# Norms of a diffusion trunk's first feed-forward block and of its mixing's input, set in steps among matrix products, with three modulations computed earlier

## The chip, the cores and the metric

The kernel runs on one core of a Trainium2 chip. The metric is the time of one execution on the device, in microseconds (us). Instructions run on five engines: TensorE (PE, matrix products; PEld is its loading of weights), VectorE (DVE), ScalarE (ACT), GpSimd (POOL) and SyncE (SP, which here issues all loads and stores, in order). Each engine executes its own list of instructions in order, and waits on semaphores for what the others make.

## The reference, cut to what matters

One layer for 1024 latent tokens and 256 context tokens, model width 1024, feed-forward width 2816:

```python
def rms_norm(x, w):
    xf = x.astype(jnp.float32)
    y = xf * lax.rsqrt(jnp.mean(xf * xf, axis=-1, keepdims=True) + EPS)
    return (y * w.astype(jnp.float32)).astype(x.dtype)

def modulate(h, shift, scale):
    return h * (1.0 + scale[:, None, :]) + shift[:, None, :]

def swiglu(h, w1, w3, w2):
    return (jax.nn.silu(h @ w1) * (h @ w3)) @ w2
...
m_l = jnp.split(cond_lat @ ada_w[i] + ada_b[i], N_MOD, axis=-1)
m_c = jnp.split(cond_ctx @ ada_w[i] + ada_b[i], N_MOD, axis=-1)
x = x + 0.5 * m_l[2] * swiglu(modulate(rms_norm(x, norm1_w[i]), m_l[0], m_l[1]), ffn1_w1[i], ffn1_w3[i], ffn1_w2[i])
ctx = ctx + 0.5 * m_c[2] * swiglu(modulate(rms_norm(ctx, norm1_w[i]), m_c[0], m_c[1]), ffn1_w1[i], ffn1_w3[i], ffn1_w2[i])
y_l, y_c = token_mixing(modulate(rms_norm(x, norm2_w[i]), m_l[3], m_l[4]),
                        modulate(rms_norm(ctx, norm2_w[i]), m_c[3], m_c[4]), w_in[i], ...)
x = x + m_l[5] * y_l
x = x + 0.5 * m_l[8] * swiglu(modulate(rms_norm(x, norm3_w[i]), m_l[6], m_l[7]), ffn2_w1[i], ffn2_w3[i], ffn2_w2[i])
return rms_norm(x, final_norm_w)
```

`m_l` and `m_c` hold nine modulations of 1024 values each, for latent and context tokens. The context needs modulations 0 to 4 alone; the latents use 5 on the way out of the mixing, 6 and 7 in the norm before the second feed-forward block (FFN2), and 8 in FFN2.

## The kernel before

All arithmetic is in float32. Each operand of a product is split into a high and a low part (`split`: ACT makes the high part, L58, DVE or POOL subtracts it, L59), and each product is three matmuls: high by high, low by high and high by low (`mm3`, L63 to L65). Weights come through a ring of six raw tiles (NR), loaded at L232, and a ring of six pairs `whi`, `wlo` (NH). Activations lie transposed, features over the 128 partitions, tokens along the row: x as eight tiles k of 128 features for each token group, which are latent half 0, latent half 1 (512 tokens each) and the context (256).

The first feed-forward block (FFN1) of the latents uses a scheme of seven products in place of eight for each 2 by 2 block of matrices. **Phase 1** (`hidden`, up to about 475 us) makes the hidden tiles, two of the 22 at a time, in chains of seven products of 12 matmuls, and writes seven combinations of them to memory. Between the chains it computes modulations (`mods`, MPER reductions a time): a column of a modulation is one load of 512 KB (`ada`) and one reduction on DVE over 1024 values (L104), with low priority in the scheduler, for latents and context alike when both need it. Modulations 0 and 1 of the latents are done by the start, and phase 1 makes 2, 4 and 3 for both and 1 and 0 for the context.

The **second phase** (`back6`, up to about 690 us) reads these combinations (`gd`) and weights (`w2` blocks, or sums of them, `sd`) back. It does products 1, 2, 6, 5, 7 and 3, in this order, of eleven steps each; a step is 12 matmuls of 512 columns with one pair of split operands (`whi`, `wlo` for the weights, `hh`, `hl` for the activations) into four banks of PSUM (`psa` or `psb`). Products 7 and 3 of these subtract two loaded blocks on DVE first (L364). Each step calls the generator `feed` once. `feed` loads the context's x in the first eight steps, then the latents' x again, one tile each two steps (L1354), and from the second quarter of x on also makes modulations 5, 7 and 6 in halves (`mods_half`): 24 columns in two halves of 512, each a strided load of 256 KB (L118) and a reduction (L119). After product 2 the function `ctx_in` norms the context, with its two norm matmuls lowered by 300 (LR1), so that they stand behind product 6 on PE.

A norm is: `squares` (ACT squares, L151 and L154; DVE adds up in `nacc`, L155), `rstd_col` (one narrow matmul for each 128 tokens sums over the partitions, L164; `pow_half` takes DVE, L913, and POOL, L914, for the power -1/2, tile `nr`), `rstd_rows` (DVE makes diagonal matrices `ndiag`, L174; a matmul with ones spreads them, L176; ACT copies, L183, tile `nrb`), and `norm_k` for each of the eight tiles (L191 on DVE, L192 on ACT, L193 on DVE).

Then comes the context's FFN1 in classic form (`classic`, 11 calls of two hidden tiles each, with POOL as the engine for low parts, and `Y`, which multiplies the hidden tiles back and adds to x, L531 and L544), up to about 901 us; product 4 of the latents, to 934; the context's keys and values for the mixing (`ctx_k`, `ctx_v`), to 970; then the mixing of the latents (`lat_phase`). The norms of the mixing's input lie in here: that of latent half 1 before `classic`, with a priority 100 lower for its part up to the spread, and one `norm_k` after each call of `classic`; that of the context after the last `Y`; that of latent half 0 after `ctx_k`, its `norm_k` after `ctx_v`.

The order of each engine's instructions is not that of the code alone: a scheduler places them by priority, where `high_priority` moves a stretch of the code ahead (a negative offset moves it back). `pair` and `load_half` load and split ahead of the products in this way.

## Time and profile before

| what | value |
| --- | --- |
| median of 3 runs | 2230.6 us (2229.64 to 2230.91) |
| profiled execution | 2230.59 us, its span 2228.1 us |
| mean granted PE clock | 0.989 |
| PE busy | 95% of the span, 11442 matmuls |
| DVE, ACT, POOL busy | 70%, 44%, 13% |
| HBM | 298.29 MB read, 66.09 MB written, 164 GB/s over the span |

A row of a timeline reads: start, duration, engine, line, operation, output<-inputs, shapes, how many were joined; in brackets the idle time of the engine before it and what released it. A row of the waits reads: engine, tile and line that waited, <- what it waited for: us in total, how many times, the longest. Matmul records overlap, so that their pace is read from start to start. Line numbers are those of the kernel before; the kernel after has the same statements a few lines off (its L165 and L177 are L164 and L176 here, L60 is L59, L64 to L66 are L63 to L65, L911 is L913, L175 is L174, L105 is L104, L360 is L364, L410 is L414).

### The profile page before, as it was taken

How to read it: one execution, taken by the hardware profiler on the slowest of the kernel's cores; microseconds unless marked ns; L12 is line 12 of the kernel's file. 1: busy time of each engine (PE TensorE's matmuls, PEld its weight loads, DVE VectorE, ACT ScalarE, POOL GpSimd, SP SyncE). 2: the span in 40 equal slices, each digit the busy share in tenths (PEclk: the TensorE clock that was granted, in tenths of full speed). 3: DMA queues.
4: the chain of work that ended last, by engine and by line, in shares of the span. 5: the costliest groups of instructions: out<-in, count | busy, mean ns of one | idle time of the engine just before them, and what ended most of it. 6: DMA issues, size and time to landing. Idle time of an engine off the chain costs nothing. (4 is left out here: it accounts for less than half of the span.)

```text
span 2228.1 us, 32714 instructions
## 1 busy us (share of the span) xinstructions
PE 2121.1 (95%) x11442; PEld 1800.6 (81%) x11442; DVE 1550.9 (70%) x2803; ACT 982.5 (44%) x1807; POOL 290.1 (13%) x294
## 2 busy tenths in 40 slices
PE   4999999999798999999998999999999999999998
PEld 3877888887687999888877888778878888888888
DVE  7999986665698745763567446766786766665686
ACT  3333344344344554555653445334444343444553
POOL 2000000000003665331032112300000000010000
PEclk9999999999999999999999999999999999999999
DMA  6558654468897566554322223324234444457674
GB/s 238 184 158 274 216 174 139 142 220 272 289 342 242 167 184 189 178 181 112 99 65 73 78 78 88 101 74 158 79 123 146 161 153 154 147 199 249 210 247 150
DMA packets 206822, 374.95 MB, mean 168 GB/s; under 512 B 24321, under 2 KB 37569, under 8 KB 206657
## 3 DMA queue, kind: packets, MB, share of 16 engines
q1 hardware_dynamic: 206656, 372.86, 51.7%
q8 instruction: 89, 1.46, 0.3%
q14 instruction: 77, 0.62, 0.1%
HBM read 298.29 MB, written 66.09 MB: 164 GB/s over the span
## 5 line engine op out<-in xcount | busy, mean ns | idle before, releaser
L58 ACT ACTIVATE whi<-raw 128x512 fp32r<-128x512 f32 (+1 forms) x659 | 406.6, 623 | 726.7 <-issue 219.3
L59 DVE TENSOR_TENSOR wlo<-raw,whi 128x512 fp32r<-128x512 f32 (+1 forms) x541 | 376.1, 698 | 312.3 <-ACT whi L58 305.1
L63 PE MATMUL psa<-hh,whi 128*128 128x512 f32 (+1 forms) x1432 | 526.7, 369 | 8.2 <-ACT hh L192 6.1
L65 PE MATMUL psa<-hh,wlo 128*128 128x512 f32 (+1 forms) x1432 | 527.0, 368 | 4.0 <-DVE wlo L59 2.1
L64 PE MATMUL psa<-hl,whi 128*128 128x512 f32 (+1 forms) x1432 | 527.7, 368 | 3.2 <-DVE hl L59 2.7
L63 PEld LDWEIGHTS psa<-hh,whi 128*128 128x128 f32 x1432 | 272.1, 190 | 51.7 <-ACT hh L192 7.2
L64 PEld LDWEIGHTS psa<-hl,whi 128*128 128x128 f32 x1432 | 272.6, 190 | 47.3 <-DVE hl L59 5.2
L65 PEld LDWEIGHTS psa<-hh,wlo 128*128 128x128 f32 x1432 | 272.5, 190 | 45.9 <-DVE wlo L59 2.5
L63 PE MATMUL psb<-hh,whi 128*128 128x512 f32 (+1 forms) x740 | 283.5, 385 | 6.8 <-ACT whi L58 2.5
L65 PE MATMUL psb<-hh,wlo 128*128 128x512 f32 (+1 forms) x740 | 284.0, 384 | 1.5 <-DVE wlo L59 1.5
L64 PE MATMUL psb<-hl,whi 128*128 128x512 f32 (+1 forms) x740 | 284.2, 384 | 0.8 <-DVE hl L59 0.8
L59 POOL TENSOR_TENSOR wlo<-raw,whi 128x512 fp32r<-128x512 f32 (+1 forms) x118 | 159.2, 1368 | 199.2 <-ACT whi L58 196.5
L63 PEld LDWEIGHTS psb<-hh,whi 128*128 128x128 f32 x740 | 139.5, 189 | 37.1 <-ACT whi L58 4.2
L65 PEld LDWEIGHTS psb<-hh,wlo 128*128 128x128 f32 x740 | 139.3, 188 | 30.6 <-DVE wlo L59 3.7
L64 PEld LDWEIGHTS psb<-hl,whi 128*128 128x128 f32 x740 | 139.6, 189 | 29.2 <-DVE hl L59 2.4
L914 POOL TENSOR_TENSOR nr<-nr,mhalf 128x4 f32<-128x4 f32 (+1 forms) x11 | 10.6, 963 | 883.8 <-DVE nr L913 880.7
L59 DVE TENSOR_TENSOR hl<-raw,hh 128x512 fp32r<-128x512 f32 x159 | 109.5, 694 | 9.8 <-ACT hh L58 9.5
L58 ACT ACTIVATE hh<-raw 128x512 fp32r<-128x512 f32 x159 | 97.0, 620 | 18.9 <-DMA raw<-gd 16.4
L64 PE MATMUL psa<-wlo,hh 128*128 128x256 f32 (+1 forms) x320 | 94.2, 294 | 0.2
L63 PE MATMUL psa<-whi,hh 128*128 128x256 f32 (+1 forms) x320 | 93.5, 292 | 0.0
L65 PE MATMUL psa<-whi,hl 128*128 128x256 f32 (+1 forms) x320 | 92.9, 290 | 0.0
L64 PEld LDWEIGHTS psa<-wlo,hh 128*128 128x128 f32 x320 | 62.2, 195 | 1.0 <-DVE wlo L59 0.9
(360 smaller groups left out, 3656.4 us busy)
## 6 DMA issues: line engine op xcount, KB each, us to landing
raw<-in_w SPq DMA_DIRECT2D x374, 256.0 KB, 3.1
gd<-s SPq DMA_DIRECT2D x154, 256.0 KB, 3.0
raw<-gd SPq DMA_DIRECT2D x154, 256.0 KB, 3.8
ada<-in_adaT SPq DMA_DIRECT2D x56, 512.0 KB, 4.3
s<-in_w SPq DMA_DIRECT2D x66, 256.0 KB, 4.5
s<-in_adaT SPq DMA_DIRECT2D x64, 256.0 KB, 5.1
sd<-s SPq DMA_DIRECT2D x44, 256.0 KB, 2.8
hh<-in_w SPq DMA_DIRECT2D x44, 256.0 KB, 4.5
```

The source lines that it names most:

```text
L58: nc.scalar.activation(hi, src, AF.Copy)
L59: (eng or nc.vector).tensor_tensor(out=lo, in0=src, in1=hi.bitcast(F32), op=ALU.subtract)
L63: mm(ps, wa[0], xa[0], start=start, stop=False, skip_group_check=more)
L64: mm(ps, wa[0], xa[1], start=False, stop=False, skip_group_check=more)
L65: mm(ps, wa[1], xa[0], start=False, stop=stop, skip_group_check=more)
L914: nc.gpsimd.tensor_tensor(out=r, in0=r, in1=self.mhalf[:, :n], op=ALU.pow)
```

## The change

Modulations 5, 7 and 6 join the list of phase 1 as 24 reductions of full width, and MPER goes from 4 to 6; the second phase makes none. `feed` follows a plan by step number: loads of x at the same steps as before, and steps of the norms. A norm is cut into steps: 0 the squares, 1 `rstd_col`, 2 `rstd_rows` with the copy, and one `norm_k` each. The context's first norm has its steps at 22 (the first of product 6, counted from 0), 24, 27 and 30 to 37; the second norm of latent half 1 has its squares before `classic` and one step after each of its calls; the last `Y` of the context's FFN1 and the context's second norm lie inside product 4, at its steps 1, 4, 6, 7 and 8; that of latent half 0 has its squares after product 4 and its next two steps inside `ctx_k`. The lowered priorities of these norms go. Product 4 uses the banks `psa` instead of `psb`, and the transposes of the gate columns in `ctx_v` get priority 60 lower.

```diff
-    def back6(self, mid=lambda: None, keep=True):
+    def back6(self, keep=True):
...
         self.add4(0, 0, self.plus4(c1, B))
-        mid()
         self.prod(6, A, False)
...
+        plan = defaultdict(list)
+        for k in range(KD):
+            plan[k].append(lambda k=k: self.load_x((None, None, hc), (2,), (k,)))
+        for i, (tg, k) in enumerate((tg, 4 * q + k) for tg, q in ((0, 0), (1, 1), (0, 1), (1, 0)) for k in range(4)):
+            o = TGS[tg][0]
+            plan[8 + 2 * i].append(lambda tg=tg, k=k, o=o: nc.sync.dma_start(self.x[tg][k], I["xT"][k * P:(k + 1) * P, o:o + 512]))
+        nrm = {}
+
+        def norm_step(tg, i, a, b):
+            n = TGS[tg][1]
+            if i == 0:
+                nrm[tg] = self.squares(self.x[tg], n, n2)
+            elif i == 1:
+                nrm[tg] = self.rstd_col(nrm[tg], n, n2)
+            elif i == 2:
+                pr = self.rstd_rows(nrm[tg], n, n2)
+                nrm[tg] = self.scr(n2, "nrb")[:, :n]
+                nc.scalar.copy(nrm[tg], pr)
+            else:
+                self.norm_k(tg, i - 3, a, b, nrm[tg], n2)
+
+        ctx1 = lambda i: norm_step(2, i, self.mcol(1, 1), self.mcol(0, 1))
+        norm2 = lambda tg, i: norm_step(tg, i, self.mcol(4, int(tg == 2)), self.mcol(3, int(tg == 2)))
+        for i, at in enumerate((22, 24, 27, *range(30, 30 + KD))):
+            plan[at].append(lambda i=i: ctx1(i))
+
+        CT = [(2, 0, 256)]
+        p4 = 6 * NP
+        plan[p4 + 1] += [lambda: self.Y(NF - 2, CT), lambda: self.alloc_h((2,), hc), lambda: norm2(2, 0)]
+        plan[p4 + 4].append(lambda: norm2(2, 1))
+        plan[p4 + 6].append(lambda: norm2(2, 2))
+        for k in range(KD):
+            plan[p4 + 7 + k // 4].append(lambda k=k: norm2(2, 3 + k))
+
         def feed():
-            for k in range(KD):
-                self.load_x((None, None, hc), (2,), (k,))
-                yield
-            late = self.mods_half(hc, LMODS)
-            for i, (tg, q) in enumerate(((0, 0), (1, 1), (0, 1), (1, 0))):
...
-        def ctx_in():
-            self.psN = self.psB
-            self.norm_mod(2, self.mcol(1, 1), self.mcol(0, 1), n2, LR1)
-
-        self.back6(ctx_in, False)
+            for i in range(7 * NP):
+                for go in plan[i]:
+                    go()
+                yield
+
+        self.feed = feed()
+        self.psN = self.psB
+        self.back6(False)
...
+        self.alloc_h((1,), self.hp)
+        norm2(1, 0)
+        pend = [lambda i=i: norm2(1, i) for i in range(1, 3 + KD)] + [lambda: spill(1)]
         for f in range(0, NF, 2):
             self.classic(f, (2,), mid=(lambda: self.Y(f - 2, CT)) if f else None, eng=[nc.gpsimd if e else None for e in CENG])
-            for _ in range(NPEND if f else 0):
-                if pend:
-                    pend.pop(0)()
-        self.Y(NF - 2, CT, after)
-        B = self.bank4(self.psB)
-        self.prod(4, B, True)
-        self.add4(0, 1, B)
-        after(0, 0, 512)
+            pend.pop(0)()
+        A = self.bank4(self.psA)
+        self.prod(4, A, True)
+        self.add4(0, 1, A)
+        self.alloc_h((0,), self.hp)
+        norm2(0, 0)
+        for i, _ in enumerate(self.ctx_k(f1)):
+            if i in (3, 5):
+                norm2(0, i // 2)
+        self.ctx_v(f1)
+        for k in range(KD):
+            norm2(0, 3 + k)
+        spill(0)
...
-EMODS = ((2, (0, 1)), (1, (1,)), (0, (1,)), (4, (0, 1)), (3, (0, 1)))
-LMODS = (5, 7, 6)
-MPER = 4
-LR1 = 300
+EMODS = ((2, (0, 1)), (1, (1,)), (0, (1,)), (4, (0, 1)), (3, (0, 1)), (5, (0,)), (7, (0,)), (6, (0,)))
+MPER = 6
...
-RP = (0, 100, 0)
-NPEND = 1
```

PE at the context's first norm, before: the last matmul of a step of product 6 (`psa`), the two norm matmuls (`psb` from `nacc` and from `ndiag`; one record stands for two), and the next step, of product 5 (`hh`, `hl` activations, `whi`, `wlo` weights).

```order
2302 L65 MATMUL psa_4066<-hh_1102_5004,wlo_5013 128x512
2303 L164 MATMUL psb_4682<-ones_88,nacc_4659 128x1 x2
2304 L176 MATMUL psb_4688<-ndiag_4689,ones_88 128x128
2305 L63 MATMUL psb_5040<-hh_1117_5044,whi_5052 128x512
2306 L64 MATMUL psb_5040<-hl_1118_5045,whi_5052 128x512
2307 L65 MATMUL psb_5040<-hh_1117_5044,wlo_5053 128x512
```

L164 and L176 are neighbours. After, the first norm matmul follows a step of product 6:

```order
2205 L65 MATMUL psa_4139<-hl_1048_4784,whi_4791 128x512
2206 L66 MATMUL psa_4139<-hh_1047_4783,wlo_4792 128x512
2207 L165 MATMUL psb_4808<-ones_88,nacc_4736 128x1 x2
2208 L64 MATMUL psa_4136<-hh_1055_4814,whi_4822 128x512
2209 L65 MATMUL psa_4136<-hl_1056_4815,whi_4822 128x512
2210 L66 MATMUL psa_4136<-hh_1055_4814,wlo_4823 128x512
```

and the second one stands 36 product matmuls further on, three steps later:

```order
2241 L64 MATMUL psa_4139<-hh_1067_4863,whi_4871 128x512
2242 L65 MATMUL psa_4139<-hl_1068_4864,whi_4871 128x512
2243 L66 MATMUL psa_4139<-hh_1067_4863,wlo_4872 128x512
2244 L177 MATMUL psb_4887<-ndiag_4888,ones_88 128x128
2245 L177 MATMUL psb_4887<-ndiag_4891,ones_88 128x128
2246 L64 MATMUL psa_4136<-hh_1077_4896,whi_4904 128x512
2247 L65 MATMUL psa_4136<-hl_1078_4897,whi_4904 128x512
```

The two matmuls, adjacent before, have three steps between them now.

DVE at the same place, before: `nr` and `ndiag` are the norm's, `wlo` and `hl` low parts for steps to come, L119 the half reductions.

```order
773 L119 ISA modl_80 128x1
774 L59 TENSOR_TENSOR wlo_5163<-raw_5160,whi_5162 128x512
775 L59 TENSOR_TENSOR hl_1132_5100<-raw_5101,hh_1131_5099 128x512
776 L913 TENSOR_SCALAR nr_4685<-psb_4682 128x2
777 L174 TENSOR_SCALAR ndiag_4689<-ident_92,nr_4685 128x128
778 L174 TENSOR_SCALAR ndiag_4692<-ident_92,nr_4685 128x128
779 L59 TENSOR_TENSOR wlo_5190<-raw_5187,whi_5189 128x512
780 L59 TENSOR_TENSOR hl_1139_5127<-raw_5128,hh_1138_5126 128x512
781 L119 ISA s_5029,modl_80<-s_5029,row_4508,cols_78 128x512
782 L119 ISA modl_80 128x1
```

After, with L360 a subtraction of weight blocks for product 7, and L410 the addition of product 2 to x:

```order
774 L60 TENSOR_TENSOR wlo_4930<-raw_4927,whi_4929 128x512
775 L60 TENSOR_TENSOR hl_1068_4864<-raw_4865,hh_1067_4863 128x512
776 L410 SCALAR_TENSOR_TENSOR x_862_4123<-s_4425,modl_80,x_862_4123 128x512
777 L360 TENSOR_TENSOR hh_1203_5371<-hh_1203_5371,hl_1204_5373 128x512
778 L911 TENSOR_SCALAR nr_4811<-psb_4808 128x2
779 L360 TENSOR_TENSOR hh_1210_5398<-hh_1210_5398,hl_1211_5400 128x512
780 L60 TENSOR_TENSOR wlo_4954<-raw_4951,whi_4953 128x512
781 L60 TENSOR_TENSOR hl_1078_4897<-raw_4898,hh_1077_4896 128x512
782 L175 TENSOR_SCALAR ndiag_4888<-ident_92,nr_4811 128x128
783 L175 TENSOR_SCALAR ndiag_4891<-ident_92,nr_4811 128x128
```

The half reductions are gone; `nr` stands behind splits, an addition and a subtraction, and `ndiag` behind one subtraction and two splits more.

PE at the end of the context's FFN1, after: the last hidden-tile matmul of `classic` (`psa` 256 wide), and then product 4 (`hh`, `hl` activations, 512 wide); 24 rows of it stand ahead of the last `Y` (`ghi`, `glo`, row 4267).

```order
4241 L65 MATMUL psa_8678<-hl_858_4119,whi_8674 128x256
4242 L66 MATMUL psa_8678<-hh_857_4118,wlo_8675 128x256
4243 L64 MATMUL psa_8716<-hh_1965_8720,whi_8728 128x512
4244 L65 MATMUL psa_8716<-hl_1966_8721,whi_8728 128x512
4245 L66 MATMUL psa_8716<-hh_1965_8720,wlo_8729 128x512
```

```order
4264 L64 MATMUL psa_8719<-hh_1971_8744,whi_8752 128x512
4265 L65 MATMUL psa_8719<-hl_1972_8745,whi_8752 128x512
4266 L66 MATMUL psa_8719<-hh_1971_8744,wlo_8753 128x512
4267 L64 MATMUL psb_8780<-ghi_8623,whi_8770 128x256
4268 L65 MATMUL psb_8780<-glo_8624,whi_8770 128x256
```

Before, the last `Y` came first and product 4 behind it.

Two further places in words. On PE the first norm matmul of latent half 1 moves from row 2825, behind the first matmuls of the second call of `classic`, to row 2798, right behind the first call, and the second one from rows 2835 to 2840 to rows 2943 to 2957. For latent half 0 the first norm matmul moves from rows 4585 to 4592, among `ctx_v`'s products, to row 4522, among `ctx_k`'s, and the second one from row 4599 to row 4571; the context's second norm has rows 4351 and 4376, inside product 4. On DVE the 24 new reductions stand in rows 483 to 602, behind all earlier ones. SP loses the 48 strided loads, and gets 24 loads of 512 KB earlier.

## Prediction

> **What bounds the kernel now.** I read the page's busy times first, then the busy time by stage (windows), then the timeline where a stage shows TensorE (PE) idle, and last the waits of the engine that released it.

> ```profile
> PE 2121.1 (95%) x11442; PEld 1800.6 (81%) x11442; DVE 1550.9 (70%) x2803; ACT 982.5 (44%) x1807; POOL 290.1 (13%) x294
> ```

> PE is busy 2121.1 of 2228.1 us. The change removes no product, so it can win only PE's idle time, and the slow clock that follows idle time. The windows tell where that lies (columns: stretch, length, PE, weight load, DVE, ACT and POOL busy, granted clock, DMA share, GB/s).

> ```profile
> 200.00:310.00 110.00, 110.00 (x484) 90.39 (x483) 108.55 (x181) 42.72 (x75) 0.00 (x0) 1.00 0.70 224
> 316.00:393.00 77.00, 77.00 (x342) 63.75 (x341) 49.62 (x78) 31.27 (x55) 0.00 (x0) 1.00 0.44 143
> 526.00:543.00 17.00, 14.78 (x61) 11.45 (x62) 8.28 (x13) 7.93 (x16) 0.00 (x0) 1.00 0.81 254
> 543.00:587.00 44.00, 40.41 (x167) 30.56 (x167) 31.39 (x63) 16.61 (x29) 0.00 (x0) 1.00 0.87 287
> 587.00:610.00 23.00, 13.67 (x56) 11.14 (x56) 12.71 (x31) 7.52 (x15) 0.70 (x1) 0.78 0.90 314
> 610.00:690.00 80.00, 78.83 (x341) 63.30 (x340) 76.87 (x155) 37.65 (x69) 0.86 (x1) 1.00 0.92 325
> 690.00:755.00 65.00, 56.59 (x420) 53.87 (x419) 56.39 (x76) 34.34 (x65) 40.27 (x27) 0.95 0.54 172
> 890.00:915.00 25.00, 22.73 (x126) 19.54 (x125) 19.91 (x42) 15.69 (x33) 0.70 (x1) 0.93 0.60 188
> 950.00:968.00 18.00, 16.25 (x117) 15.71 (x116) 11.03 (x15) 9.83 (x22) 9.87 (x9) 0.91 0.55 177
> ```

> Phase 1 (the first two rows) keeps PE full. From 526 on PE is idle 2.22, 3.59, 9.33, 1.17, 8.41, 2.27 and 1.75 us, 28.7 us together; this is nearly all that the change can touch. The largest piece is the context's first norm, which the scheduler put between products 6 and 5 of the second phase. Its timeline:

> ```profile
> 587.27 0.50 PE L164 MATMUL psb<-ones,nacc 128*128 128x1 f32 x4
> ...
> 593.34 0.75 DVE L119 CUSTOM_DVE_ANT_0 s<-s,row,cols 128x512 f32<-128x512 f32 x1 [2.50 <-DMA s<-in_adaT]
> ...
> 594.01 0.69 DVE L59 TENSOR_TENSOR wlo<-raw,whi 128x512 fp32r<-128x512 f32 x1
> ...
> 595.22 0.15 DVE L913 TENSOR_SCALAR nr<-psb 128x2 f32<-128x2 f32 x1
> ...
> 595.51 0.70 POOL L914 TENSOR_TENSOR nr<-nr,mhalf 128x2 f32<-128x2 f32 x1 [542.08 <-DVE nr L913]
> ...
> 596.25 0.48 DVE L174 TENSOR_SCALAR ndiag<-ident,nr 128x128 f32<-128x128 f32 x2 [0.87 <-POOL nr L914]
> ...
> 596.59 0.80 PE L176 MATMUL psb<-ndiag,ones 128*128 128x128 f32 x2 [8.81 <-DVE ndiag L174]
> ...
> 597.61 0.63 PE L64 MATMUL psb<-hl,whi 128*128 128x512 f32 x1
> ...
> 598.04 0.63 PE L65 MATMUL psb<-hh,wlo 128*128 128x512 f32 x1
> ```

> L164 sums the squares; L176 spreads the result over the partitions; they are neighbours on PE. Between them DVE needs only 0.15 + 0.48 us and POOL 0.70, but L913 stands on DVE behind half reductions (L119), of which one waits 2.50 us for its load, and behind splits (L59). So PE waits 8.81 us. After that the matmuls start 0.43 us apart (597.61, 598.04); the usual step is 110.00 us / 484 = 0.227 us (row 200:310).

> The same reductions hold up splits earlier in the phase:

> ```profile
> 551.42 0.75 DVE L119 CUSTOM_DVE_ANT_0 s<-s,row,cols 128x512 f32<-128x512 f32 x1 [2.62 <-DMA s<-in_adaT]
> ...
> 553.45 0.50 PE L64 MATMUL psa<-hl,whi 128*128 128x512 f32 x1 [0.84 <-DVE hl L59]
> ```
> ```profile
> DVE s L119 <- DMA s<-in_adaT: 13.9, 8, 2.7
> ```
> ```profile
> L119 DVE CUSTOM_DVE_ANT_0 s<-s,row,cols x32: 743/747/754, 543.6 to 1819.4; 128x512 f32<-128x512 f32 x32
> ```

> DVE waits 2.62 us for a modulation's load while the split that PE needs stands behind; PE loses 0.84 us. In 526 to 690 DVE waits so 13.9 us in 8 times. The first L119 runs at 543.6, so the 2.22 us of 526:543 have another cause.

> **The change part by part.** The profiled execution took 2230.59 us, 2.5 us more than its span; the median of the runs shown is 2230.6, so I take the sums from 2230.6.

> *Modulations out of the second phase.* 48 halves go: 48 x 0.75 = 36 us of DVE and 12.6 MB of loads, of 210 us, together with DVE's waits for them. Splits are then queued behind splits only. In 543:587 I give back 3.0 of 3.59 us; in 610:690, where DVE is at 76.87 of 80, 0.8 of 1.17; in 526:543 only 0.5 of 2.22. Bounds for these three: nothing, and 7.0.

> *Modulations into phase 1.*

> ```profile
> L104 DVE CUSTOM_DVE_ANT_0 junk<-ada,condc,cols x40: 1273/1280/2317, 8.0 to 311.0; 128x1024 bf16<-128x1024 f32 x40
> ...
>   DMA ada<-in_adaT: 9.9, 5
> ```

> 24 full reductions x 1.28 us = 30.7 us. The new program's order puts them on DVE behind the last old ones (311.0), among the rows that ran from 316 to 393, where DVE was busy 49.62 of 77 us: 80.3 us of work, so DVE falls 3.3 us behind there. What covers this is the lead of the splits: a ring of six weight pairs, each used for 12 matmuls x 0.227 = 2.7 us, lets DVE be up to five pairs, 13.6 us, ahead. In 200:310 DVE was 108.55 of 110 us busy with the same mix and PE lost nothing. The loads add 24 x 0.52 MB = 12.6 MB in 77 us, 163 GB/s on top of 143: 306, between 224 (no loss) and the 325 of 610:690 (1.17 us lost in 80). I charge 1.0 us; bounds 0 and the rate of 526:587, 5.81 lost in 61, so 7.3. If the cover were gone, each microsecond of DVE would be one of PE.

> *Context's first norm.* It is put in steps among those of product 6. In the new order 36 matmuls stand between the two norm matmuls: 36 x 0.227 = 8.2 us of cover for 0.15 + 0.70 + 0.48 us of norm. On DVE, though, nr still has four instructions ahead of it that no longer wait on modulations, and ndiag three more: seven x 0.7 = 4.9. With 0.14 us of handing over at each of two changes of engine (595.37 to 595.51) that makes 6.5 us, within the cover. But two of the seven are splits of weights for later steps, which wait for their loads, and a late load cost 2.5 to 2.6 us above: with one late, 6.5 + 2.6 - 8.2 = 0.9 us of the wait is left, with both 3.5. I leave 2.0; bounds 0 and 9.33. The eight modulated tiles that follow are the same instructions as before, now one per step of a product (2.7 us); DVE, 31.39 of 44 us busy in 543:587, has room for them. The slow clock behind the wait:

> ```profile
> 597.00:600.00 3.00, 3.00 (x9) 2.42 (x9) 1.60 (x4) 0.00 (x0) 0.00 (x0) 0.50 0.87 262
> 704.00:716.00 12.00, 6.82 (x37) 5.81 (x38) 9.25 (x11) 6.46 (x14) 5.94 (x5) 0.86 0.71 244
> 897.00:899.00 2.00, 2.00 (x12) 2.00 (x11) 1.63 (x5) 1.02 (x3) 0.00 (x0) 0.50 0.88 302
> ```

> 3 us at half speed lose 1.5. I leave half of that too. Gain: 9.33 + 1.5 - 2.0 - 0.7 = 8.1 us.

> *Latent half 1's second norm, at the start of the context's FFN.*

> ```profile
> 704.76 0.39 PE L63 MATMUL psa<-hh,whi 128*128 128x256 f32 x1 [0.81 <-ACT whi L58]
> 706.24 0.39 PE L65 MATMUL psa<-hh,wlo 128*128 128x256 f32 x1 [0.97 <-POOL wlo L59]
> 710.40 0.39 PE L63 MATMUL psa<-hh,whi 128*128 128x256 f32 x1 [1.00 <-ACT whi L58]
> 711.76 0.38 PE L65 MATMUL psa<-hh,wlo 128*128 128x256 f32 x1 [0.86 <-POOL wlo L59]
> 713.72 1.86 PE L164 MATMUL psb<-ones,nacc 128*128 128x1 f32 x8 [1.57 <-DVE nacc L155]
> ```
> ```profile
> 705.53 1.20 DVE L155 TENSOR_TENSOR nacc<-nacc,nsq 128x512 f32<-128x512 f32 x1 [0.47 <-ACT nsq L154]
> 706.66 2.39 DVE L59 TENSOR_TENSOR wlo<-raw,whi 128x512 fp32r<-128x512 f32 x2
> ...
> 711.92 1.75 DVE L155 TENSOR_TENSOR nacc<-nacc,nsq 128x512 f32<-128x512 f32 x1
> ```

> Five waits, 5.2 us. In the new order the first norm matmul comes 27 rows sooner, right behind the first pair of f, so PE reaches it about 703.9 (704.76 - 0.81) and stands there until nacc is summed, with all further products queued behind it. nacc's last addition has one split ahead instead of four, so I put it at 709 instead of 713.7: one wait of 5 us in which ACT, DVE and POOL run ahead and the four product waits vanish. Gain 0.7 with the tail of the 8.41 us unchanged; bounds: -4.5 (nacc still at 713.7: 9.7 us against 5.2) and +8.4. The second norm matmul follows 145 rows later, which covers it.

> The clock here: the granted clock is 0.86 in 704:716, behind waits of at most 1.57 us; 897:899 runs at 0.50 behind one wait of 1.91 us (below). [...]

> *End of the context's FFN.*

> ```profile
> 895.70 0.74 PE L63 MATMUL psb<-ghi,whi 128*128 128x256 f32 x4 [1.91 <-ACT ghi L58]
> ```

> PE waits for the last hidden tile. The new order puts two steps of product 4 (24 matmuls, 5.4 us) ahead of that last Y, and the context's second norm later in product 4, with 25 matmuls between its two matmuls. Of 2.27 us idle and 1.5 of slow clock I give back 3.4. Bounds 0 and 3.8. If ACT fell 5.4 us behind, the wait would be back.

> *Latent half 0's second norm.*

> ```profile
> 934.55 5.80 DVE L155 TENSOR_TENSOR nacc<-nacc,nsq 128x512 f32<-128x512 f32 x4
> ```
> ```profile
> 954.46 0.16 DVE L913 TENSOR_SCALAR nr<-psb 128x4 f32<-128x4 f32 x1 [14.10 <-PE psb L164]
> ```
> ```profile
> 957.07 0.71 PE L176 MATMUL psb<-ndiag,ones 128*128 128x128 f32 x4 [1.75 <-DVE ndiag L174]
> ```

> nacc is ready at 940.4, yet DVE waits 14.10 us for L164, since that stands late on PE; then PE waits 1.75. Now 49 matmul rows lie between the two matmuls, about 49 x 0.13 (56.59 us / 420 in 690:755) = 6.4 us, against 954.46 to 957.07 = 2.6. Of 1.75 and 18 x 0.09 = 1.6 of slow clock I give back 3.2. POOL's power stands behind context-key splits; were that late by 4 us, the wait would return. Bounds 0 and 3.4.

> **Sum:** 0.5 + 3.0 + 0.8 + 8.1 + 0.7 + 3.4 + 3.2 - 1.0 = 18.7, so 2230.6 - 18.7 = 2211.9 us. Behind 968 us the products stand in the same order as before.

> **The rivals.** About 0.2%, 4.5 us, is what a measurement of this kernel can tell from no change.

> (a) *The context norm still waits.* nr and ndiag remain behind splits whose loads land late, and PE stands at the second matmul as before. For: 314 GB/s and 0.90 of DMA in 587:610. Against: a cover of 8.2 us. 18.7 - 8.1 = 10.6 gained: 2220.0. Chance 0.20.

> (b) *The second phase is bound by its loads.* The stalls of 526 to 690 are those of rings that wait for transfers, as 526:543 shows without any modulation, and the classic start pays its bound: 18.7 - 0.5 - 3.0 - 0.8 - 8.1 - 5.2 = 1.1: 2229.5. Against: 12.6 MB fewer in 210 us. Chance 0.11.

> (c) *Phase 1 becomes bound by DVE.* Each of the 24 full reductions stands on DVE for its 512 KB load, with the splits behind it. In before five waited 9.9 us, 2.0 each. If all 24 do, DVE stands 48 us more; with 3.3 behind and 13.6 us of lead that leaves 37.7 us on PE. The other gains are 19.7 without the 1.0 charged here: 2230.6 - 19.7 + 37.7 = 2248.6. It decides, against the other gains, from 24 x 1.25 us on (13.6 + 19.7 - 3.3 = 30 us). For: 306 GB/s where DVE has no slack. Against: at the 325 GB/s of 610:690 the loads keep up. Chance 0.05.

> (d) *The classic start clears as well*, since DVE enters it without a backlog: 8.41 idle and 1.7 of clock (12 us x 0.14), less the 0.7 counted: 9.4 more, 2202.5. Chance 0.08.

> That leaves 0.56 for the forecast, 2212. The range runs from (d) to 2225: it holds (a) and the half of the classic-start bound, and leaves out (b) and (c), 0.16. Faster: 0.56 + 0.20 + 0.08 = 0.84; same 0.11; slower 0.05.

> **What would show it.** Right: no wait over 2.5 us in the second phase; no L119 before 1000 us; PE full from 316 to 393; the waits at 895.70 and 957.07 gone; one wait of about 5 us in the classic start. Wrong: PE idle in 300 to 470; a wait at the context norm's second matmul of over 5 us; the 526 to 690 stretch still losing 7 us.

## The result, and the profile after

| | us | ratio to before, 95% interval |
| --- | --- | --- |
| before, beside the first reading | 2230.1 (2225.5 to 2230.9) | |
| changed, first reading | 2210.5 (2208.8 to 2213.1) | 0.9917 [0.9900, 0.9934] |
| changed, a second reading, beside a before of 2230.0 | 2208.1 (2203.3 to 2210.5) | 0.9894 [0.9878, 0.9910] |

The change wins about 20 us. The prediction was 2212, range 2202 to 2225, so its total and its direction hold. How the total comes together is another matter, as the stretches show.

The changed kernel's page, busy times, and its windows (stretch, length, PE, weight load, DVE, ACT, POOL busy, clock, DMA share, GB/s):

```profile
PE 2116.0 (96%) x11442; PEld 1796.9 (81%) x11442; DVE 1548.0 (70%) x2755; ACT 980.2 (44%) x1805; POOL 290.0 (13%) x294
```
```profile
316.00:393.00 77.00, 76.95 (x339) 62.93 (x338) 74.46 (x125) 27.90 (x49) 0.00 (x0) 1.00 0.85 284
...
526.00:543.00 17.00, 14.32 (x60) 10.81 (x59) 8.17 (x14) 8.72 (x18) 0.00 (x0) 1.00 0.83 265
543.00:587.00 44.00, 41.80 (x180) 32.53 (x180) 26.19 (x45) 16.68 (x30) 1.01 (x1) 1.00 0.90 290
587.00:610.00 23.00, 21.96 (x93) 16.80 (x92) 15.73 (x31) 14.17 (x29) 0.00 (x0) 1.00 0.73 232
610.00:690.00 80.00, 80.00 (x379) 67.25 (x378) 59.22 (x91) 37.70 (x68) 9.62 (x8) 1.00 0.76 245
690.00:755.00 65.00, 60.29 (x469) 59.16 (x468) 50.09 (x78) 35.12 (x66) 39.97 (x28) 0.95 0.53 161
```

The 9.33 us of idle PE in 587:610 are 1.04 now; the transfers of 526 to 587 are as dense as before (0.83 to 0.90), and DVE in 316:393 went from 49.62 to 74.46 us busy. The context's norm has moved forward to 568 us. Its timeline in the changed kernel:

```profile
568.07 0.50 PE L165 MATMUL psb<-ones,nacc 128*128 128x1 f32 x4
...
575.25 0.15 DVE L911 TENSOR_SCALAR nr<-psb 128x2 f32<-128x2 f32 x1
...
577.12 0.47 DVE L175 TENSOR_SCALAR ndiag<-ident,nr 128x128 f32<-128x128 f32 x2
...
577.45 0.71 PE L177 MATMUL psb<-ndiag,ones 128*128 128x128 f32 x4 [0.52 <-DVE ndiag L175]
```

From the first norm matmul to the second it takes 9.38 us, as in the kernel before (587.27 to 596.59, 9.32): the chain is no shorter. But 8.2 us of it is now covered by 36 product matmuls, and PE waits 0.52 us instead of 8.81.

Since the time of day shifts, stretches are best compared by the number of the matmul: the table gives, in us, the time between the starts of the matmul records with these numbers (both kernels have 11442, with the same products in the same order but for the 24 of product 4 and the norm matmuls).

| matmul records | what lies there | before | changed, 1st and 2nd profile | won | forecast |
| --- | --- | --- | --- | --- | --- |
| 0 to 1300 | start, phase 1 (the new reductions begin near its end, at 313 us) | 324.9 | 327.0, 325.2 | -2.1, -0.2 | 0 |
| 1300 to 2000 | phase 1 with the new reductions | 158.7 | 160.8, 160.6 | -2.1, -2.0 | -1.0 |
| 2000 to 2400 | products 2 and 6, context norm | 111.4 | 100.2, 97.5 | 11.2, 13.9 | 11.6 |
| 2400 to 2800 | products 5, 7, 3 | 85.8 | 83.0, 83.0 | 2.7, 2.8 | 0.8 |
| 2800 to 3200 | start of classic | 61.7 | 57.0, 57.0 | 4.7, 4.7 | 0.7 |
| 3200 to 4200 | classic | 120.0 | 120.0, 120.0 | 0 | 0 |
| 4200 to 4500 | end of classic, product 4 | 54.9 | 54.2, 52.6 | 0.8, 2.4 | 3.4 |
| 4500 to 5000 | ctx_k's end, ctx_v | 70.0 | 68.9, 68.5 | 1.2, 1.6 | 3.2 |
| 5000 to 11380 | same code | 1205.7 | 1203.8, 1205.5 | 1.9, 0.1 | 0 |

Profiles differ by up to 2 us where the code is the same (the two profiles of the changed kernel in the first and last row), so a single profile settles no term below that. Where a stretch has the same value in many kernels (82.98 us for 2400 to 2800, in seven of them), it is PE's own time, without any wait.

Idle time says less than such a table. The record of a 512-wide matmul lasts 0.39 to 0.50 us, but the starts are 0.227 us apart when nothing waits; a short delay is hidden under the record before it, and a longer one costs more than the idle time in brackets. So what a stall costs is counted below from start to start, as what a step takes above 0.227 us.

### The profile page after: what moved, and what is told of

Read it like the earlier page. It is cut to its first block, busy times and chain, and to the rows that moved or that the text cites. A ratio compares the mean times of both kernels' runs of the same rounds, so it can differ in the third digit from the quotient of the medians.

```text
span 2211.3 us, 32718 instructions
## 1 busy us (share of the span) xinstructions
PE 2116.0 (96%) x11442; PEld 1796.9 (81%) x11442; DVE 1548.0 (70%) x2755; ACT 980.2 (44%) x1805; POOL 290.0 (13%) x294
## 5 line engine op out<-in xcount | busy, mean ns | idle before, releaser
L59 ACT ACTIVATE whi<-raw 128x512 fp32r<-128x512 f32 (+1 forms) x659 | 406.3, 623 | 721.8 <-issue 198.8
L64 PE MATMUL psa<-hh,whi 128*128 128x512 f32 (+1 forms) x1476 | 544.6, 370 | 9.4 <-ACT hh L193 6.7
L65 PE MATMUL psa<-hl,whi 128*128 128x512 f32 (+1 forms) x1476 | 544.5, 369 | 1.2 <-DVE hl L60 0.7
L66 PE MATMUL psa<-hh,wlo 128*128 128x512 f32 (+1 forms) x1476 | 543.7, 368 | 1.8 <-DVE wlo L60 1.8
L64 PEld LDWEIGHTS psa<-hh,whi 128*128 128x128 f32 x1476 | 280.6, 190 | 55.4 <-ACT hh L193 7.9
L66 PEld LDWEIGHTS psa<-hh,wlo 128*128 128x128 f32 x1476 | 281.0, 190 | 45.2 <-DVE wlo L60 2.3
L65 PEld LDWEIGHTS psa<-hl,whi 128*128 128x128 f32 x1476 | 280.8, 190 | 45.3 <-DVE hl L60 1.8
L64 PE MATMUL psb<-hh,whi 128*128 128x512 f32 (+1 forms) x696 | 267.1, 385 | 4.7 <-ACT hh L59 2.5
L65 PE MATMUL psb<-hl,whi 128*128 128x512 f32 (+1 forms) x696 | 267.2, 384 | 1.8 <-DVE hl L60 1.8
L66 PE MATMUL psb<-hh,wlo 128*128 128x512 f32 (+1 forms) x696 | 266.7, 383 | 1.0 <-DVE wlo L60 1.0
L64 PEld LDWEIGHTS psb<-hh,whi 128*128 128x128 f32 x696 | 131.1, 188 | 33.2 <-ACT hh L59 4.7
L65 PEld LDWEIGHTS psb<-hl,whi 128*128 128x128 f32 x696 | 131.3, 189 | 29.0 <-DVE hl L60 3.8
L912 POOL TENSOR_TENSOR nr<-nr,mhalf 128x4 f32<-128x4 f32 (+1 forms) x11 | 11.6, 1057 | 868.1 <-DVE nr L911 864.4
L59 ACT ACTIVATE hh<-raw 128x512 fp32r<-128x512 f32 x159 | 97.3, 619 | 20.0 <-DMA raw<-gd 17.0
L65 PE MATMUL psa<-wlo,hh 128*128 128x256 f32 (+1 forms) x320 | 93.3, 291 | 1.6 <-DVE wlo L60 1.6
L64 PE MATMUL psa<-whi,hh 128*128 128x256 f32 (+1 forms) x320 | 93.3, 291 | 1.2 <-ACT s L866 1.2
L105 DVE CUSTOM_DVE_ANT_0 junk<-ada,condc,cols 128x1024 bf16<-128x1024 f32 x64 | 82.8, 1294 | 9.6 <-DMA ada<-in_adaT 9.2
```

The source lines that it names most:

```text
L59: nc.scalar.activation(hi, src, AF.Copy)
L64: mm(ps, wa[0], xa[0], start=start, stop=False, skip_group_check=more)
L65: mm(ps, wa[0], xa[1], start=False, stop=False, skip_group_check=more)
L66: mm(ps, wa[1], xa[0], start=False, stop=stop, skip_group_check=more)
L105: nc.vector.tensor_tensor_reduce(out=self.junk, in0=t, in1=self.cs[s], scale=1.0, scalar=self.col("ada_b")[:, j:j + 1], op0=ALU.mult, op1= ...
L912: nc.gpsimd.tensor_tensor(out=r, in0=r, in1=self.mhalf[:, :n], op=ALU.pow)
```

## The experiments

Each kernel was timed beside the kernel before on the same chip, which took 2232.2 us (median) beside e1 to e4, 2232.0 beside e5 to e8 and 2230.0 beside the others; what is compared across these groups is compared by the ratio. "Stretch A" is matmuls 2000 to 2400.

| kernel | median us | ratio, 95% interval | stretch A |
| --- | --- | --- | --- |
| e1_mods_only | 2226.8 | 0.9972 [0.9960, 0.9983] | 108.1 |
| e2_steps_only | 2226.8 | 0.9974 [0.9964, 0.9984] | 107.2 |
| e3_ctx_adjacent | 2211.0 | 0.9900 [0.9885, 0.9915] | 100.8 |
| e4_lat1_block | 2213.4 | 0.9917 [0.9902, 0.9931] | 96.8 |
| e5_end_block | 2210.4 | 0.9899 [0.9881, 0.9917] | 96.4 |
| e6_lat0_block | 2207.9 | 0.9896 [0.9877, 0.9915] | 97.7 |
| e7_no_x_loads | 2202.7 | 0.9871 [0.9850, 0.9891] | 94.0 |
| e8_adj_no_x | 2213.5 | 0.9915 [0.9897, 0.9932] | 101.1 |
| e10_ctx_block | 2217.0 | 0.9941 [0.9927, 0.9955] | 107.0 |
| e11_mods_ctx | 2215.9 | 0.9936 [0.9920, 0.9952] | 99.9 |
| e12_late_x | 2213.6 | 0.9928 [0.9912, 0.9943] | 97.0 |
| a2_changed_again | 2208.1 | 0.9894 [0.9878, 0.9910] | 97.5 |

My theory was a sum of separate gains; the rivals, that either the moved modulations or the steps make all of it.

**One part of the change alone.** e1, against the kernel before:

```diff
-            late = self.mods_half(hc, LMODS)
+            late = iter(())
...
-EMODS = ((2, (0, 1)), (1, (1,)), (0, (1,)), (4, (0, 1)), (3, (0, 1)))
-MPER = 4
+EMODS = ((2, (0, 1)), (1, (1,)), (0, (1,)), (4, (0, 1)), (3, (0, 1)), (5, (0,)), (7, (0,)), (6, (0,)))
+MPER = 6
```

> The kernel before with one part of the change alone: modulations 5, 7 and 6 move from the second phase to phase 1 (six reductions a call); all norms stay as before. My theory is that the gain is a sum over separate places: the second phase's splits gain about 4 us, the context norm's wait shrinks from 8.8 to 3 to 5 us because no half reduction stands ahead of nr on DVE any more but splits still do, phase 1 gives back 1 to 2.7 us, and the classic start, its end and ctx_v stay as before: 2220 to 2225 us, 5 to 10 under before. Rival 1, the moved modulations are the whole gain and the steps do nothing: 2209 to 2213. Rival 2, the steps are the whole gain: 2228 or more.

e2, against the changed kernel:

```diff
+        late = self.mods_half(hc, (5, 7, 6))
...
                 for go in plan[i]:
                     go()
+                for _ in range(1 if 16 <= i < 40 else 2 if i >= 40 else 0):
+                    next(late, None)
...
-EMODS = (..., (5, (0,)), (7, (0,)), (6, (0,)))
-MPER = 6
+EMODS = (...)
+MPER = 4
```

> The changed kernel with one part undone: the modulations 5, 7 and 6 are computed in halves in the second phase again, at the steps where they were, and phase 1 makes four reductions a call; the norms stay in steps. My theory: the context norm has 36 matmuls of cover, but nr and ndiag are again behind half reductions that wait for their loads, so a wait of 2 to 5 us stays; the classic start, its end and ctx_v keep their gains of together some 6 us; phase 1 has no loss: 2216 to 2222 us. Rival 1 (modulations are all): 2227 or more. Rival 2 (steps are all): 2208 to 2213.

Each wins only 5.4 us; together they win 20 to 22. Both times lie outside of my ranges, by 1.8 and 4.8 us; e2 comes within 0.2 us of its first rival (2227 or more), but e1 stays 14 us away from the same rival's 2213. So both rivals fall, and so does my plain sum: the parts need each other. The norm's two matmuls say where. e1 (modulations moved, norm as before), on PE and on DVE:

```profile
590.09 0.50 PE L164 MATMUL psb<-ones,nacc 128*128 128x1 f32 x4
...
593.25 0.69 DVE L59 TENSOR_TENSOR wlo<-raw,whi 128x512 fp32r<-128x512 f32 x1 [2.98 <-ACT whi L58]
...
597.05 0.15 DVE L913 TENSOR_SCALAR nr<-psb 128x2 f32<-128x2 f32 x1
...
598.41 0.79 PE L176 MATMUL psb<-ndiag,ones 128*128 128x128 f32 x2 [7.83 <-DVE ndiag L174]
```

e2 (norm in steps, half reductions where they were), on PE and on DVE:

```profile
564.33 0.50 PE L165 MATMUL psb<-ones,nacc 128*128 128x1 f32 x4
...
574.88 0.74 DVE L120 CUSTOM_DVE_ANT_0 s<-s,row,cols 128x512 f32<-128x512 f32 x1
...
575.55 0.15 DVE L911 TENSOR_SCALAR nr<-psb 128x2 f32<-128x2 f32 x1
...
579.06 0.74 DVE L120 CUSTOM_DVE_ANT_0 s<-s,row,cols 128x512 f32<-128x512 f32 x1
...
581.27 1.22 PE L177 MATMUL psb<-ndiag,ones 128*128 128x128 f32 x4 [6.66 <-DVE ndiag L175]
```

Without half reductions but without cover, the chain takes 8.32 us and nearly all of it is waited for (I had expected 3 to 5 us; taking the reductions out of DVE's list shortens it by 1.0 us only, since DVE still does the splits of later steps first, and waits for their high parts from ACT, once for 2.98 us). With 36 matmuls of cover but the reductions (L120) back, it takes 16.94 us, and 6.66 are left. Only both leave 0.5.

**The context norm's distance.** e3, against the changed kernel:

```diff
-        for i, at in enumerate((22, 24, 27, *range(30, 30 + KD))):
+        for i, at in enumerate((22, 24, 24, *range(30, 30 + KD))):
```

> The changed kernel with the second step of the context's first norm given out at the same step of the plan as the first (24 instead of 27): 12 product matmuls stand between its two norm matmuls instead of 36, and everything else is the same. If the distance is what removed the wait, PE waits as long as the chain over DVE took in the changed kernel, 9.4 us, less the 2.7 us of 12 matmuls: 5 to 7 us, and some clock, so 2215 to 2219 us. If the moved modulations removed it (nr comes early now), the wait stays under 1.5 us and the time within 2 us of the changed kernel's 2210.5.

```profile
561.22 0.50 PE L165 MATMUL psb<-ones,nacc 128*128 128x1 f32 x4
...
571.18 1.22 PE L177 MATMUL psb<-ndiag,ones 128*128 128x128 f32 x4 [6.75 <-DVE ndiag L175]
```

The wait came, 6.75 us, as 9.96 us of chain less the cover of 12 matmuls give it; the time did not: 0.9900 against 0.9917 and 0.9894 for the changed kernel. In stretch A it has 100.8 us where the six profiles with the changed kernel's norm there (the changed kernel twice, e4, e5, e6, e11) have 96.4 to 100.2, 98.1 in the mean: 2.7 us lost, less than half of the wait. Neither this nor its forecast time (2215 to 2219) shows in the median of 2211.0.

**The context norm's place.** e10, against the changed kernel:

```diff
-        for i, at in enumerate((22, 24, 27, *range(30, 30 + KD))):
-            plan[at].append(lambda i=i: ctx1(i))
+        def ctx_in():
+            nrm[2] = self.rstd(self.x[2], CTX, n2, 300)
+            for k in range(KD):
+                ctx1(3 + k)
...
-        self.back6(False)
+        self.back6(False, ctx_in)
```

> The changed kernel with one part undone: the context's first norm is given out in one block after product 2 with its norm matmuls 300 lower, as before, so that they are neighbours on PE between products 6 and 5; modulations stay in phase 1, the other norms in steps. Theory: moved modulations and this norm's steps need each other (36 matmuls of cover are enough for a chain over DVE of 9.4 us, not for the 15 us it takes among half reductions; and without cover the 9.4 us are all waited for). Then undoing the norm's steps alone brings a wait of about 8 us back and some slow clock: 2218 to 2224. Rival: the other steps make the gain together, each covering for the other when one is undone: 2209 to 2214.

```profile
592.49 0.80 PE L177 MATMUL psb<-ndiag,ones 128*128 128x128 f32 x2 [6.73 <-DVE ndiag L175]
```

2217.0 against 2208.1 for the changed kernel on the same chip: 8.9 us more, 1 us less than the low end of my range, and stretch A 9.5 longer. The rival (the other steps stand in for it) falls. A wait of the same size, 6.7 us, costs 9.5 us here and 2.7 in e3. In e3 it falls into the part of stretch A where the changed kernel has many small waits for splits; whether these are what it replaces, the next two kernels ask.

**Whether transfers set the rest of stretch A.** e7, against the changed kernel (e8 is the same edit on e3):

```diff
-            plan[8 + 2 * i].append(lambda tg=tg, k=k, o=o: nc.sync.dma_start(self.x[tg][k], I["xT"][k * P:(k + 1) * P, o:o + 512]))
+            plan[8 + 2 * i].append(lambda tg=tg, k=k, o=o: nc.gpsimd.memset(self.x[tg][k], 1.0))
```

> The changed kernel with the 16 loads of the latents' x in the second phase (4.2 MB) left out: POOL, idle there, fills the tiles with ones instead; the output is not the reference's. Theory: between 515 and 605 us the second phase is bound by its loads (ACT's splits wait for some 41 us there on transfers, in the changed kernel and in the one with the adjacent norm matmuls alike), so any wait of PE there is only a stall in another place. Then fewer loads shorten the stretch: 2203 to 2207. Rival: the stalls left there are chains over ACT and DVE and not transfers: within 1.5 us of the changed kernel.

> The kernel with the context norm's steps at the same step of the plan (12 matmuls between its norm matmuls, a wait of 6.75 us) and the 16 x loads left out as in the kernel next to it; the output is not the reference's. If the wait of 6.75 us cost nothing since loads ran ahead during it, then with loads no longer the bound it must show: 3 to 7 us slower than the kernel without x loads and with 36 matmuls between. Rival: the chain gets shorter without loads and the two are equal within 1.5 us.

e7 is 5 to 8 us faster than e5 and e6 beside it (the intervals of the ratios overlap), in stretch A 2.4 us faster than e5 and 3.7 than e6, so 4.2 MB of loads seem to hold up the products there. e8 is 10.8 us slower than e7, above my 3 to 7, with 7.0 in stretch A and 2.4 at the start of classic:

```profile
569.54 0.79 PE L177 MATMUL psb<-ndiag,ones 128*128 128x128 f32 x2 [5.01 <-DVE ndiag L175]
```

Its wait of 5.01 us now costs all of itself and more. The comparison is not clean: the scheduler left 4 matmuls ahead of its second norm matmul, not the 12 of e3, and the chain took 6.5 us instead of 10. And one of my signs was none: ACT's waits on transfers from 515 to 605, of which I had made an argument, are as long in e7,

```profile
ACT whi L59 <- DMA raw<-sd: 22.8, 18, 2.2
ACT whi L59 <- DMA raw<-in_w: 18.5, 9, 4.7
```

41.3 us, as in the changed kernel (41.2), though PE waits less. They are idle time of an engine that is ahead.

What the records do settle is where each kernel loses time in stretch A. The table counts it from start to start: the norm's matmuls with their wait and the slow clock right behind it, and what all other steps take above 0.227 us, ahead of the norm and behind it, in us.

| kernel | norm | other stalls ahead of it | other stalls behind it |
| --- | --- | --- | --- |
| before | 12.6 | 10.0 | 0.3 |
| e1 | 12.1 | 7.5 | 0.2 |
| e10 | 11.5 | 6.9 | 0.2 |
| e3 | 9.9 | 2.6 | 0.0 |
| changed, 1st and 2nd profile | 2.2, 2.2 | 7.1, 4.8 | 2.5, 2.2 |
| e7 | 1.4 | 4.2 | 0.0 |
| e8 | 8.8 | 4.1 | 0.0 |

The norm in one block (before, e1, e10) stands behind nearly all other stalls, so its wait can replace none of them and costs its full price. In e3 it stands further ahead, and behind it no step is late any more, where the changed kernel loses 2.2 to 2.5 us: that much the wait replaces. e7 loses nothing there either, and ahead of the norm it loses what the others do: as far as one profile shows, the loads of x make the stalls behind the norm and no others of stretch A. The smaller loss ahead of the norm in e3, 2.6 us against 3.4 to 7.1 in the six profiles above, can't be made by a wait that comes later, and its cause stays open; with a loss there like theirs, e3 would have been some 5 us behind the changed kernel in stretch A.

**Spreading these loads.** e12, against the changed kernel:

```diff
+        def late_x(tg, k, o):
+            if (tg, k // 4) != (0, 0):
+                nc.gpsimd.tensor_copy(out=self.x[tg][k][:, 0:1], in_=self.cur[0].bitcast(F32)[:, 0:1])
+            nc.sync.dma_start(self.x[tg][k], I["xT"][k * P:(k + 1) * P, o:o + 512])
...
-            plan[8 + 2 * i].append(...)
+            plan[8 + 2 * i if i < 4 else 28 + 2 * (i - 4)].append(lambda tg=tg, k=k, o=o: late_x(tg, k, o))
```

> The changed kernel with 12 of the 16 loads of the latents' x held back: each waits for a one-column copy on POOL from the split activations of a step (steps 28 to 50 of the plan, two apart; before 16 to 38, and the scheduler let them run ahead), so that product 2 and the start of product 6 share the DMA engines with 12 loads fewer. Without any x load the stretch of products 2 and 6 took 3 to 6 us less and the run about 8. If the loads' bunching is the bound, half of that comes: 2204 to 2208. Rival: the held-back loads only move the bound into products 5 and 7: 2209 to 2213.

Slower, 2213.6 against 2208.1: the rival holds, 0.6 us above its range. Stretch A is unchanged at 97.0, and the next one went from 83.0 to 90.3:

```profile
635.21 0.50 PE L65 MATMUL psa<-hl,whi 128*128 128x512 f32 x1 [2.12 <-DVE hl L60]
...
651.04 0.50 PE L65 MATMUL psa<-hl,whi 128*128 128x512 f32 x1 [1.78 <-DVE hl L60]
```

There DVE's subtraction of weight blocks waits longer for its loads, beside which the late ones now run, and the splits behind it on DVE are late. The subtraction's waits for loads of weights in this stretch, products 5, 7 and 3, come to 18.9 us, against 4.4 in a2_changed_again. The waits of e12 from 625 to 655:

```profile
DVE hh L360 <- DMA hh<-in_w: 14.3, 6, 4.0
```

So removing the loads helps in stretch A, and moving them so does not.

**The other steps, undone one at a time.** All against the changed kernel. e4, latent half 1's second norm:

```diff
-        norm2(1, 0)
-        pend = [lambda i=i: norm2(1, i) for i in range(1, 3 + KD)] + [lambda: spill(1)]
+        with tc.high_priority(offset=-100):
+            for i in range(3):
+                norm2(1, i)
+        spill(1)
+        pend = [lambda: None] + [lambda i=i: norm2(1, i) for i in range(3, 3 + KD)] + [lambda: None] * 2
```

> The changed kernel with the second norm of latent half 1 given out as before: squares and both norm matmuls ahead of classic with a priority 100 lower, its eight tiles from the second call on. The trace of the changed kernel gained 4.7 us between the classic start and 755 us where I had forecast 0.7. If the place of the two norm matmuls made this, the waits of 704 to 714 us come back and the time is 2213 to 2217. If DVE entering classic without a backlog of reductions made it, the time stays within 1.5 us of the changed kernel.

e5, the last Y and the context's second norm:

```diff
-        plan[p4 + 1] += [lambda: self.Y(NF - 2, CT), lambda: self.alloc_h((2,), hc), lambda: norm2(2, 0)]
-        plan[p4 + 4].append(lambda: norm2(2, 1))
-        plan[p4 + 6].append(lambda: norm2(2, 2))
...
+        self.alloc_h((2,), hc)
+        self.Y(NF - 2, CT, lambda tg, o, n: after())
-        A = self.bank4(self.psA)
+        A = self.bank4(self.psB)
```

> The changed kernel with one part undone: the last Y of the context's FFN1 stands ahead of product 4 again, and the context's second norm behind it, ahead of product 4's end as before. I had forecast 3.4 us for this part; the traces so far show 0.8 to 2.5 us between rows 4200 and 4500 with it and 0.4 without it (modulations alone). If the forecast was right in size, 2213 to 2214; if later waits on the same context additions ate the gain, 2210 to 2212, within 1.5 us of the changed kernel, with the wait of 1.9 us on the last hidden tile back.

e6, latent half 0's second norm:

```diff
-        norm2(0, 0)
-        for i, _ in enumerate(self.ctx_k(f1)):
-            if i in (3, 5):
-                norm2(0, i // 2)
+        for _ in self.ctx_k(f1):
+            pass
+        for i in range(3):
+            norm2(0, i)
         self.ctx_v(f1)
```

> The changed kernel with one part undone: the norm of latent half 0 up to its spread stands behind all of ctx_k again instead of inside it. Forecast 3.2 us; the traces with this part show about 1 us won between rows 4500 and 5000, the kernel with the moved modulations alone shows 1.9 lost. If the part carries its forecast, 2213 to 2214. If the wait at the norm only becomes waits of ctx_v's products on copies and splits that now share DVE and ACT with the norm's tiles, 2210 to 2212.

None of the three differs from the changed kernel beyond its interval. By stretches: e4 takes 58.7 us at the start of classic where the changed one takes 57.0, so the steps are worth 1.7 there and the rest of the change 3.0. e5 takes 55.4 in 4200 to 4500, against 52.6 and 54.2, with its wait on the hidden tile back:

```profile
875.80 0.38 PE L64 MATMUL psb<-ghi,whi 128*128 128x256 f32 x1 [2.36 <-ACT ghi L59]
```

e6 takes 67.9 in 4500 to 5000 against 68.5 and 68.9, although its norm waits again:

```profile
933.30 0.46 PE L177 MATMUL psb<-ndiag,ones 128*128 128x128 f32 x2 [1.37 <-DVE ndiag L175]
```

**Two parts alone.** e11 is e1 with the context norm's eleven steps called from `feed`, at the changed kernel's step numbers, and nothing else of the change:

```diff
+        at = {s: i for i, s in enumerate((22, 24, 27, *range(30, 30 + KD)))}
...
+                if s in at:
+                    ctx1(at[s])
                 yield
...
-        self.back6(ctx_in, False)
+        self.psN = self.psB
+        self.back6(keep=False)
```

> The kernel before with two parts of the change alone: modulations 5, 7 and 6 in phase 1, and the context's first norm in steps inside product 6; the norms of the mixing's input, the last Y and product 4 stay as before. Theory: these two are nearly the whole gain, since undoing each of the other parts cost nothing: 2209 to 2214. Rival (the other steps together carry half of it, hidden from kernels that undo only one): 2216 to 2220.

2215.9: 14 of the 22 us that the changed kernel wins beside it, 1.9 us beyond my range and at the edge of the rival's. Against a2_changed_again it loses 2.3 us at the start of classic (59.3), 2.0 in 4200 to 4500 (54.6) and 3.2 in 4500 to 5000 (71.7): 7.5, close to the 7.8 between the medians. (The profiled execution of e11 took 3.5 us more than its median, and loses 2.4 more in stretch A, where its code is that of the changed kernel.) So the rest of the change together does carry a third of the gain, though I could not see its parts one at a time.

a2_changed_again is the changed kernel once more:

> The changed kernel unchanged, once more, so that the three others of this call and the earlier ones have a reading on the same chip: by all theories a ratio to the kernel before of 0.989 to 0.993. The traces of four kernels with the same code in products 2 to 6 spread over 4 us there; this one shows whether the first profile (100.2 us for that stretch, the others 96.4 to 97.7) was the odd one.

Its ratio of 0.9894 lies in the range, and with 97.5 us in stretch A it makes the first profile the odd one there.

## Why the prediction was right in its total, step by step

*Context's first norm: right in mechanism, its size too small.* Forecast 2.0 us of wait left, found 0.5. The cover of 36 x 0.227 = 8.2 us was the right term to count. The chain I put at 6.5 to 9.1 us took 9.4. Stretch A won 11.2 and 13.9 us against 11.6, but by the table of its losses the norm won 10.5 of that (8.1 forecast), and the splits' stalls 0.7 and 3.4 (3.5 forecast, 0.5 + 3.0): that the sum fits so well is luck. What I left out is that the gain stands on two parts at once; my rival (a) asked about late loads, where the real danger was the half reductions, and e2 shows what it costs with them: 6.66 us.

*Modulations out of the second phase: too small in products 5, 7 and 3.* 0.8 was forecast, 2.7 found, against an idle time of 1.17 that I took as the bound. It is no bound: the two waits that make up most of it in the kernel before,

```profile
679.84 0.50 PE L63 MATMUL psb<-hh,whi 128*128 128x512 f32 x1 [0.64 <-ACT whi L58]
...
681.04 0.50 PE L65 MATMUL psb<-hh,wlo 128*128 128x512 f32 x1 [0.47 <-DVE wlo L59]
```

start 1.02 and 0.87 us after the matmul before them in place of 0.227, and with the smaller delays around them, from 676 to 686, the steps above 0.227 us add up to 2.5. In e2, with reductions, the stretch takes 88.3.

*Start of classic: the step that failed.* I wrote one wait of 5 us in place of five, a gain of 0.7, and gave a chance of 0.08 to DVE entering classic without a backlog. The changed kernel:

```profile
697.33 0.83 PE L165 MATMUL psb<-ones,nacc 128*128 128x1 f32 x6 [1.85 <-DVE nacc L156]
...
741.65 0.38 PE L64 MATMUL psb<-ghi,whi 128*128 128x256 f32 x1 [2.09 <-ACT ghi L59]
```

e2, with the steps and with reductions until then:

```profile
709.58 0.58 PE L165 MATMUL psb<-ones,nacc 128*128 128x1 f32 x2 [5.45 <-DVE nacc L156]
```

DVE's first additions to nacc, in the changed kernel and in e2:

```profile
688.67 4.89 DVE L156 TENSOR_TENSOR nacc<-nacc,nsq 128x512 f32<-128x512 f32 x4
```
```profile
699.24 5.19 DVE L156 TENSOR_TENSOR nacc<-nacc,nsq 128x512 f32<-128x512 f32 x3
```

They begin 3.7 us ahead of matmul 2800 in the changed kernel (and 3.8 in e1), but 1.9 ahead of it in e2 and in the kernel before, although no reduction runs from 690 to 710 us: what the reductions leave there is a backlog on DVE. My 5 us are what comes if the reductions stay: I took nacc's end from a trace in which they still delayed DVE. e1, with the old norm, takes 57.4 us there, e2 61.6: it is the moved modulations that won most of this stretch: 4.3 of 4.7 in e1, 3.0 in e4. So rival (d)'s mechanism is the one that came true, for less than half of its price (4.0 us above the forecast, of 9.4); a wait of 2.09 us at 741.65 stays.

*End of classic and ctx_v: too large.* 6.6 forecast, 2 to 4 found. The two waits that I named are gone, but others of 1.1 to 1.25 us appear in the first profile of the changed kernel (in the second, the one at 871.05 is 0.62 and the one at 891.41 is not there):

```profile
871.05 0.39 PE L64 MATMUL psb<-ghi,whi 128*128 128x256 f32 x1 [1.18 <-DVE x L539]
...
891.41 0.38 PE L64 MATMUL psb<-ghi,whi 128*128 128x256 f32 x1 [1.09 <-DVE x L539]
...
959.58 0.39 PE L64 MATMUL psa<-whi,hh 128*128 128x256 f32 x1 [1.19 <-ACT s L866]
```

Y waits for its banks to be read out by DVE, and ctx_v waits for ACT's copies, which share ACT with the norm's tiles. I had asked who hides each wait, not who comes next. Why 4500 to 5000 takes 67.9 us with e6's block, but 71.7 to 71.9 in e1 and e11, was not tried. The traces show that e6's wait is shorter (1.37 us against 1.75 in e11), and the mean granted clock over its whole profiled execution higher, 0.992 against 0.987 in e1 and 0.988 in e11; the lowered transposes of ctx_v and the other banks of product 4 are left as candidates for the cause.

*Phase 1: size 1.0, found 2.0; and the cover that I named was not the one that failed.* Splits kept their lead. a2_changed_again, ACT and DVE ahead of the one wait of PE:

```profile
390.35 0.68 DVE L280 TENSOR_TENSOR s<-psa,s 128x512 f32<-128x512 f32 x1
...
391.07 0.63 ACT L303 ACTIVATE s<-s 128x512 f32<-128x512 f32 x1 [3.62 <-DVE s L280]
...
392.12 0.57 ACT L276 COPY s<-psa 128x512 f32<-128x512 f32 x1
...
392.74 0.50 PE L64 MATMUL psa<-hh,whi 128*128 128x512 f32 x1 [1.18 <-ACT s L276]
```

DVE's addition L280 stands behind the reductions; ACT's Silu (L303) waits 3.62 us for it, and the copy that frees PE's bank (L276) stands behind the Silu on ACT. PE waits for a bank, not for a weight. Rival (c), DVE-bound phase 1, stayed far from its price.

So three terms were too small, the norm by 2.4 us, products 5, 7 and 3 by 2 and the start of classic by 4, and three were too large: the splits in stretch A by up to 2.8, the end of classic with ctx_v by 2.6 to 4.6, and, by its charge of 1 us too little, phase 1. That their sum came within 1 to 3 us of the measured gain is in good part luck; what the prediction had right is the mechanism of its largest term.

## What to carry to other kernels

To hide a chain over other engines, count the chain as it stands in their lists, with all that is queued ahead, and then the product time between its two ends; taking work out of the list or spacing the ends may each do almost nothing alone. Work that is taken off an engine also changes the state in which it enters the next stage, so a term for that stage read from the old trace can be too pessimistic, as it was here at the start of classic. Read what stalls cost from start to start: where records overlap, the idle time between them is less than what is lost (1.17 against 2.5 us here). When parts are undone one by one and each costs nothing, also build the kernel that has only the parts believed to matter: here it lacked 7.8 of 22 us.
